# Hybrid encoder step on one core: the gate chain in five pieces, the memory values later, and the last sums of squares by accumulating transfers

## Chip, cores and metric

One core of a Trainium2 chip. The metric is the time of one execution in microseconds of the device. Six engines matter: PE (TensorE: matmuls, with PEld its weight loads), DVE (VectorE), ACT (ScalarE), POOL (GpSimd) and SP (SyncE), which issues most transfers.

## What is computed

One inference step of a one-layer encoder for 512 prompt frames and 32 sample frames, T = 544 columns, D = 2048, all in float32. Cut to what matters here:

```python
z = rmsnorm(x) @ w_in                        # gb, gc, hin, q, k, v and 8 forget gates
logf = log_sigmoid(z[..., o6:] + b_f)        # cumulated over time, enters the scores
x += concat(rmsnorm(gb * conv(gc * hin)), rmsnorm(attention(q, k, v, logf))) @ w_out
mk, mv = split(rmsnorm(mem) @ w_xkv)         # 256 memory tokens
x += softmax(rmsnorm(x) @ w_xq @ mk.T * scale) @ mv @ w_xo
x += square(relu(rmsnorm(x) @ w_up)) @ w_down
y = rmsnorm(x)
```

Prompt and sample frames have their own caches; new keys, values, gates, convolution rows and memory keys and values are outputs too.

## The kernel before

Activations stand with features on the partitions and the 544 columns along the free axis, in two halves of 272. Every float32 matmul is made of three: a tile is rounded by ScalarE to `hi` (float32r), VectorE subtracts to get `lo` (`split`, L82), and hi·hi, hi·lo and lo·hi are added in PSUM. Weights come raw from HBM by SyncE (`raw`), in blocks of 128 x 1024, and are split on the way (`whi`, `wlo`, tags `hi` and `lo`, four buffers each).

The input projection (22 pairs of output blocks) and the first MLP matrix (32 pairs) use `seven` (L240): seven products of 24 matmuls, on sums of weight blocks (`combine`, VectorE, names `sum`) and on sums of column halves made beforehand by `operands` (L199: `b11`, `b21`, `b22`, `t1` to `t4`), in the order b11, t1, t2, b22, t3, b21, t4. Product b11 goes to the PSUM tile X (`mmx`), which ScalarE copies out (`p15`, L259) before t2 may accumulate further in it; t1 goes to Y (`mmy`, copied at L263).

The order of each engine's queue is the order of the program, but for two helpers: `combine` and `operand` (the split of weights) are placed 40 instructions earlier, and `rstd` at the place that a scheduler finds for it. `rstd` (L168) makes the reciprocal root of a mean square: a matmul with a constant matrix sums the tile `acc` over the partitions (`ssq`), ScalarE takes a logarithm and an exponential, and four VectorE steps refine it (`nt`, `rstd`). `square` (L185) has ScalarE square a tile, and VectorE add it to `acc` (`accumulate`, L159).

Stages, in order: head; 22 pairs of the input projection, the first ten of them convolution blocks (`hr`, `gc`, `gb`), the others keys, queries and values; attention beside half 0 of `w_out`; half 1; memory keys (L777 to 789) and values (L790 to 804); the four heads' queries and scores (L902 to 913), values (`x_transpose`, `x_values`); `w_xo` in 16 units of 128 outputs (`xo_done`, L936: add to the residual `x2r`, store, square into `acc_3`, scale by the gain, and at every second unit `operands` for the MLP); `rb_3` of `acc_3` (L1010); 32 `seven`s up; down; final norm.

Places that the change touches:

- The gates: `chain_logf` (L357) after pair 0, with the transposes `turn_logf` after pair 1. ScalarE's part of it is `e` (L365), `lf` (L367), `neg` (L380) and `ncs` (L386); VectorE's has a reciprocal (L369) and two scans (L378, L383). It uses eight rotating tiles of `tmp`.
- `rb_c`, the norm of the convolution group, made right after the last `gb` (L487).
- The memory values, made right after the keys, and each head's transposes and values (`sb`, `sc`) between the queries of the next.
- The weights of `w_xo`, split as each block is needed (L979).
- The last residual's sum of squares:

```python
        dve.tensor_tensor(two(x), two(x), ps[:, :, :TH], ALU.add)
        sp.dma_start(x3d[m], x)
        square(x, acc_3, m == order[0])
```

Of the kernel before, what the change touches and what calls it, by code (L numbers as in the profile page):

```python
# [15 lines left out]
D = 2048  # L16
# [25 lines left out]
def hybrid_step(  # L42
# [125 lines left out]
    def rstd(acc, dim, width=T, early=0):  # L168
        with tc.high_priority(offset=early):
# [29 lines left out]
    def operands(x, b11, ts, tags):  # L199
        hi, lo = two(b11)[:, 0], two(b11)[:, 1]  # L200
        split(hi, lo, x[:, 0])
        t = ts.rearrange("p (a b c) -> p a b c", a=2, b=2)
        x4 = x.rearrange("p (a b) c -> p a b c", a=2)
        dve.tensor_tensor(t[:, :, 0], x4[:, :, 1], x4[:, 0], ALU.subtract)
        for a in range(2):
            dve.tensor_tensor(t[:, a, 1], x[:, 3 - a], t[:, 0, a], ALU.subtract)
        o = {"b11": (hi, lo)}
        o["b21"], o["b22"] = both(x[:, 2:], tags[1])
        o["t1"], o["t2"] = both(t[:, 0], tags[0])
        o["t3"], o["t4"] = both(t[:, 1], tags[2])  # L210
        return o
# [28 lines left out]
    def seven(pl, ops, ws, out, scale, mid, prefetch):  # L240
# [25 lines left out]
        product(X, w, "t2", False)  # L266
        act.activation(u23[:, 0], X, AF.Copy)
# [89 lines left out]
    def chain_logf(z16):  # L357
        z, lf, e, w = tmp("z"), tmp("lf"), tmp("e"), tmp("w")
        z, lf, e, w = z[:8, :T], lf[:8, :T], e[:8, :T], w[:8, :T]
        for a in range(2):  # L360
# [13 lines left out]
        cum, lfs = tmp("cum"), tmp("lfs")  # L374
        act.dma_start(lfs[:8, :PAST], clogf)
# [98 lines left out]
    for i, pair in enumerate(pairs):  # L474
# [315 lines left out]
    ps = mm_tile()  # L790
    for p in range(8):
        hi, lo = weights(w_xv[p])
        for kk in range(2):
            k = 2 * p + kk
            c = slice(512 * kk, 512 * kk + 512)
            for t in range(2):
                d = slice(128 * t, 128 * t + 128)
                for n, (x, w) in enumerate(((mem[k][0], hi), (mem[k][0], lo), (mem[k][1], hi))):
                    pe.matmul(ps[:, t], x[:, d], w[:, c], start=k == 0 and n == 0, stop=k == KD - 1 and n == 2)  # L799
    for t in range(2):  # L800
        mf = tmp("mv")[:, :512]
        dve.tensor_scalar(mf, ps[:, t], rcol[:, t:t + 1], None, ALU.mult)
        pool.dma_start(o_mv[128 * t:128 * t + 128], mf)
        split(mvs[t][0], mvs[t][1], mf)
# [28 lines left out]
    def x_scores(h, q):  # L833
        P = xp.tile([128, 4, NMEM], F32, tag="P", name="xP")
# [19 lines left out]
    def x_transpose(h, P):  # L854
        PT = []
        for kt in range(2):
# [3 lines left out]
            hi = xp.tile([128, SEQ], F32R, tag=f"pth{kt}", name="xpth")  # L860
            lo = xp.tile([128, SEQ], F32R, tag=f"ptl{kt}", name="xptl")
# [4 lines left out]
    def x_values(h, PT):  # L866
# [51 lines left out]
    acc_3 = new_acc()  # L918
# [17 lines left out]
    def xo_done(m, ps):  # L936
# [337 lines left out]
```

## Time and profile before

| | us |
|---|---|
| three runs | 2391.26, 2392.85, 2392.91 (median 2392.85) |
| the profiled execution | 2392.07 |
| its span | 2390.3 |
| PE busy | 2325.7 (97%) |
| DVE busy | 2017.8 (84%) |
| ACT busy | 1303.1 (55%) |
| POOL busy | 197.0 (8%) |

The mean granted clock of TensorE is 0.988 of full speed. TensorE's busy time counts overlapped matmuls once; a matmul of 128 x 272 takes a new place every 0.125 us at the full clock. The gap between TensorE's busy time and the span is 64.6 us.

### The profile page before, as it was taken

Reading aid. Unit: us, or ns where it says so; the run is one execution under the profiler, and the core shown is the slowest. Engines: PE = TensorE matmul, PEld = TensorE weight load, DVE = VectorE, ACT = ScalarE, POOL = GpSimd, SP = SyncE. Lnnn points to the kernel's source line nnn. Section 1 sums busy time; section 2 is a strip of 40 time slices with the busy share of each in tenths; the row PEclk is TensorE's granted clock in tenths of the full one; section 3 lists DMA queues with packets and bytes.
Section 4 is the critical chain, followed back from the end, with each engine's and each line's share of the span. In section 5 each row is a group of like instructions: output and inputs, shape, how many; then the busy total and the mean of one; then the engine's idle time right before and its main releaser. Section 6 shows DMA issues by size and latency. Waiting matters only on the chain.

```text
span 2390.3 us, 47513 instructions
## 1 busy us (share of the span) xinstructions
PE 2325.7 (97%) x18147; PEld 2295.4 (96%) x18147; DVE 2017.8 (84%) x3561; ACT 1303.1 (55%) x2524; POOL 197.0 (8%) x382
## 2 busy tenths in 40 slices
PE   8799999999999999899999999999999999999997
PEld 8699989999999998799999999999999999999997
DVE  9888988886767665989999999998598898888887
ACT  8345445554555444756666665666255555555555
POOL 0000011112300000001111111111000000000000
PEclk9899999999999999899999999999999999999999
DMA  5323345548715453446565556565956546646524
GB/s 176 106 99 125 110 133 157 162 153 317 235 62 166 139 168 127 158 142 203 190 203 186 184 194 204 191 201 172 351 191 237 174 152 237 214 131 219 177 84 137
DMA packets 160484, 416.34 MB, mean 174 GB/s; under 512 B 19384, under 2 KB 24368, under 8 KB 160256
## 3 DMA queue, kind: packets, MB, share of 16 engines
q1 hardware_dynamic: 110752, 313.87, 39.2%
q0 software_dynamic: 44000, 90.52, 12.0%
q10 hardware_dynamic: 5504, 8.93, 1.0%
q8 instruction: 142, 2.33, 0.4%
q14 instruction: 86, 0.70, 0.1%
HBM read 319.91 MB, written 93.33 MB: 173 GB/s over the span
## 4 chain that ended last, share of the span: by engine, by line
PE 91%; DVE 5%; DMA 1%; ACT 1%; issue 1%; DVEq 0%; SPq 0%; ACTq 0%
PE mmx L247 26%; PE dx L1083 14%; PE mmy L247 13%; PE mm L120 13%; PE mm L1083 11%; PE mmz L247 7%; PE mm L1177 2%; PE mm L785 1%; PE mm L799 1%; DVE wlo L85 1%; DVE opl L85 1%; PE s L532 1%; PE mm L311 1%; PE h L311 1%; PE o L588 1%
## 5 line engine op out<-in xcount | busy, mean ns | idle before, releaser
L84 ACT ACTIVATE whi<-raw 128x512 fp32r<-128x512 f32 x668 | 420.6, 632 | 498.8 <-PE mmx L247 97.1
L84 ACT ACTIVATE whi<-sum 128x512 fp32r<-128x512 f32 x656 | 409.9, 630 | 432.4 <-PE mmx L247 205.3
L85 DVE TENSOR_TENSOR wlo<-raw,whi 128x512 fp32r<-128x512 f32 x668 | 457.0, 688 | 137.6 <-ACT whi L84 125.6
L85 DVE TENSOR_TENSOR wlo<-sum,whi 128x512 fp32r<-128x512 f32 x656 | 439.6, 685 | 77.8 <-ACT whi L84 74.9
L247 PE MATMUL mmx<-oph,whi 128*128 128x272 f32 x1296 | 375.3, 290 | 20.1 <-ACT p L259 20.1
L247 PE MATMUL mmx<-oph,wlo 128*128 128x272 f32 x1296 | 375.9, 290 | 2.3 <-DVE wlo L85 2.3
L247 PE MATMUL mmx<-opl,whi 128*128 128x272 f32 x1296 | 373.8, 288 | 0.0
L1083 PE MATMUL dx<-f,whi 128*128 128x272 f32 x1792 | 344.4, 288 | 0.0
L1083 PEld LDWEIGHTS dx<-f,whi 128*128 128x128 f32 x1792 | 281.6, 188 | 0.0
L247 PEld LDWEIGHTS mmx<-oph,whi 128*128 128x128 f32 x1296 | 246.1, 190 | 21.2 <-ACT p L259 21.2
L1083 PE MATMUL mm<-f,whi 128*128 128x272 f32 x1344 | 259.6, 288 | 0.0
L1083 PE MATMUL dx<-f,wlo 128*128 128x272 f32 x896 | 258.5, 289 | 0.0
L247 PE MATMUL mmy<-oph,whi 128*128 128x272 f32 x864 | 250.9, 290 | 1.4 <-ACT whi L84 1.4
L247 PE MATMUL mmy<-oph,wlo 128*128 128x272 f32 x864 | 250.0, 289 | 0.7 <-DVE wlo L85 0.7
L247 PE MATMUL mmy<-opl,whi 128*128 128x272 f32 x864 | 249.4, 289 | 0.0
L247 PEld LDWEIGHTS mmx<-oph,wlo 128*128 128x128 f32 x1296 | 245.4, 189 | 2.7 <-DVE wlo L85 2.7
L247 PEld LDWEIGHTS mmx<-opl,whi 128*128 128x128 f32 x1296 | 245.5, 189 | 0.0
L1083 PEld LDWEIGHTS mm<-f,whi 128*128 128x128 f32 x1344 | 210.8, 188 | 0.0
L1083 PE MATMUL mm<-f,wlo 128*128 128x272 f32 x672 | 193.4, 288 | 0.0
L1083 PEld LDWEIGHTS dx<-f,wlo 128*128 128x128 f32 x896 | 168.9, 189 | 0.0
L247 PEld LDWEIGHTS mmy<-oph,whi 128*128 128x128 f32 x864 | 164.0, 190 | 2.0 <-ACT whi L84 1.8
L247 PE MATMUL mmx<-b,whi 128*128 128x272 f32 x864 | 165.0, 288 | 0.0
(381 smaller groups left out, 5175.2 us busy)
## 6 DMA issues: line engine op xcount, KB each, us to landing
raw<-in_w_up SPq DMA_DIRECT2D x128, 512.0 KB, 3.9
raw<-in_w_dn SPq DMA_DIRECT2D x112, 512.0 KB, 4.3
f<-fd SPq DMA_DIRECT2D x196, 272.0 KB, 5.7
fd<-form POOLq DMA_DIRECT2D x168, 272.0 KB, 4.0
raw<-in_w_in SPq DMA_DIRECT2D x88, 512.0 KB, 3.8
raw<-in_w_out SPq DMA_DIRECT2D x32, 512.0 KB, 4.3
raw<-in_w_ends SPq DMA_DIRECT2D x20, 512.0 KB, 4.1
kq<-hl POOLq DMA_DIRECT2D x32, 256.0 KB, 3.0
```

The source lines that it names most:

```text
L84: act.activation(hi, src, AF.Copy)
L85: dve.tensor_tensor(lo, src, hi.bitcast(F32), ALU.subtract)
L120: pe.matmul(ps[a], w, two(x)[:, a], start=first and n == 0, stop=last and n == 2)
L247: pe.matmul(ps, a[:, c], x, start=first and j == 0 and n == 0, stop=j == 7 and n == 2, skip_group_check=not first)
L311: pe.matmul(ps[a], w[:, c], xs[a][q], start=j + i == 0 and n == 0, stop=j + i == 8 and n == 2)
L532: pe.matmul(s[:, :N], q[a][:, c], k[b][:, :N], start=n == 0, stop=n == 2)
L588: pe.matmul(o[:, 128 * kt:], a[:, c], b, start=kt == 0 and n == 0, stop=False)
L785: pe.matmul(ps[:, 0, :NMEM], w[:, c], x, start=k == 0 and n == 0, stop=k == KD - 1 and n == 2)
L799: pe.matmul(ps[:, t], x[:, d], w[:, c], start=k == 0 and n == 0, stop=k == KD - 1 and n == 2)
L1083: pe.matmul(ps, a[:, c], f[:, x], start=first and j == 0 and n == 0, stop=j == 3 and n == 2, skip_group_check=not first)
L1177: pe.matmul(ps, w[:, c], two(x)[:, a], start=k == 0 and j == 0, stop=k == 3 and j == 2)
```

## The change

1. `operands` issues the same instructions in another order.
2. The gates' chain is cut into `gate_open`, `gate_exp`, `gate_log` and `gate_close`, called after pairs 0, 1, 2 and 4. `neg` is made by VectorE instead of ScalarE, the load of the cached gates (`lfs`) is issued one piece earlier, and the tiles come from other pools (one for `z`, one of tag `acc` for `e`, one of tag `hl` for `w`).
3. `rb_c` is made after pair 13 instead of pair 9.
4. The memory values (`mem_values`) are made after all four heads' queries and scores; all transposes and values of the heads follow them, in an order in which the transposes run a head ahead.
5. Four of the eight `w_xo` blocks are loaded and split inside `mem_values` (`presplit`).
6. `acc_3` becomes two tiles. The first unit of each is squared straight into it by ScalarE; the other 14 squares go to a tile `sq`, and GpSimd issues a transfer that adds `sq` to `acc_3[i]` in SBUF (`accum_op=ALU.add`). `rstd` sums a list of tiles in PSUM (one more `ssq` matmul for each half).
7. `rb_3` is asked for inside the first hidden `seven`, through the new argument `between`, after product t2.
8. The tiles of `plain`, `forms` and the heads' outputs come from a pool `ring` of three, which lives from the cross attention to the end of the first MLP matrix.

```diff
--- before.py
+++ after.py
     def rstd(acc, dim, width=T, early=0):
+        accs = acc if isinstance(acc, list) else [acc]
         with tc.high_priority(offset=early):
             rt = npool.tile([128, T], F32, tag="rstd", name="rstd", bufs=3)
             nt = tmp("nt")
@@ -173,7 +174,8 @@
             for c in range(0, width, half):
                 d = slice(c, c + half)
                 ps = aux("ssq")
-                pe.matmul(ps[:, :half], inv[dim], acc[:, d], start=True, stop=True)
+                for n, t in enumerate(accs):
+                    pe.matmul(ps[:, :half], inv[dim], t[:, d], start=n == 0, stop=n == len(accs) - 1)
...
+    gate = {}
+
+    def gate_open(z16):
+        z = gate["z"] = npool.tile([128, T], F32, tag="rstd", name="z", bufs=3)[:8]
+        e = gate["e"] = new_acc()[:8]
         for a in range(2):
             pz = aux("pz")
             pe.matmul(pz[:8, :TH], sel16, two(z16)[:, a], start=True, stop=True)
             dve.tensor_scalar(two(z)[:, a], pz[:8, :TH], vec[:8, BF:BF + 1], None, ALU.add)
         dve.scalar_tensor_tensor(e, z, -1.0, z, ALU.mult, ALU.min)
+
+    def gate_exp():
+        e = gate["e"]
+        w = gate["w"] = pj.tile([128, T], F32, tag="hl", name="w", bufs=4)[:8]
         act.activation(e, e, AF.Exp)
         dve.tensor_scalar(w, e, 1.0, None, ALU.add)
+        gate["lfs"] = tmp("lfs")
+        act.dma_start(gate["lfs"][:8, :PAST], clogf)
...
+    def gate_log():
+        z, e, w = gate["z"], gate["e"], gate["w"]
+        lf = tmp("lf")[:8, :T]
         act.activation(lf, w, AF.Ln)
         dve.scalar_tensor_tensor(e, w, -1.0, e, ALU.add, ALU.subtract)
         dve.reciprocal(w, w)
...
-        dve.tensor_tensor_scan(cum[:8, :SEQ], one, lf[:, :SEQ], 0.0, ALU.mult, ALU.add)
-        neg = tmp("neg")[:8, :SEQ]
-        act.activation(neg, cum[:8, :SEQ], AF.Copy, scale=-1.0)
-        pool.dma_start(ncd, neg)
-        cs = tmp("cs")
-        dve.tensor_tensor_scan(cs[:8, :LS], ones.to_broadcast([8, LS]), lfs[:8, :LS], 0.0, ALU.mult,
+        cum = gate["cum"] = gate["z"]
+        neg = gate["e"]
+        dve.tensor_tensor_scan(cum[:, :SEQ], one, lf[:, :SEQ], 0.0, ALU.mult, ALU.add)
+        dve.tensor_scalar(neg[:, :SEQ], cum[:, :SEQ], -1.0, None, ALU.mult)
+        pool.dma_start(ncd, neg[:, :SEQ])
...
+    def gate_close():
+        cs = gate["w"]
...
+        turn_logf(gate["cum"])
...
-        if i == 0:
-            cum = chain_logf(z16)
-        if i == 1:
-            turn_logf(cum)
+        if i < 5:
+            (lambda: gate_open(z16), gate_exp, gate_log, lambda: None, gate_close)[i]()
         if n2 == "gb" and j2 == 7:
             pool.dma_start(o_conv, newc)
+        if i == len(pairs) - 9:
             rb_c = rstd(acc_c, DC)
...
         product(X, w, "t2", False)
+        if between:
+            between()
...
+    def mem_values():
...
+            if 2 <= p < 6:
+                wos.append(presplit(w_xo[p - 2]))
...
+    def presplit(src):
+        raw = raw_block(src, None, "raw")
+        his, los = [], []
+        for c in range(0, 1024, 512):
+            hi, lo = slot("B", F32R, "woh")[:, :512], slot("C", F32R, "wol")[:, :512]
+            split(hi, lo, raw[:, c:c + 512])
+            his.append(hi)
+            los.append(lo)
+        return Parts(his), Parts(los)
...
     for h in range(HX):
         qs[h] = evac_xq(h, xq(h))
-        if h == HX - 1:
-            Pss = xs_scores()
-            sa(h)
-            sb(h - 1)
-            sc(h - 1)
+        sa(h)
+    Pss = xs_scores()
+    mem_values()
+    for h in range(HX):
+        if h < 3:
+            o = ring("o")
+            ox.append((flat(o[:, 0]), flat(o[:, 1])))
         else:
-            sa(h)
-            if h < HX - 2:
-                sb(h)
-                sc(h)
+            ox.append([npool.tile([128, T], F32R, tag="rstd", name="o", bufs=3) for n in range(2)])
...
-    acc_3 = new_acc()
+    acc_3 = [new_acc(), new_acc()]
...
-        square(x, acc_3, m == order[0])
         j, i = m % 8, m // 8
+        if j == 0:
+            act.activation(acc_3[i], x, AF.Square)
+        else:
+            sq = tmp("sq")[:, :T]
+            act.activation(sq, x, AF.Square)
+            pool.dma_start(acc_3[i], sq, accum_op=ALU.add)
...
+    sb(0)
     PTs = samp_transpose(xp, Pss, NMEM)
+    sb(1)
+    sc(0)
     osx = samp_values(xp, PTs, cmvt, None)
+    sb(2)
+    sc(1)
     ot = samp_out(osx)
     for i in range(HX):
         split(ox[i][0][:, SEQ:], ox[i][1][:, SEQ:], ot[:, 32 * i:32 * i + 32])
-    order = [m for j in range(8) for m in (j, j + 8)]
-    wo = None
+    sb(3)
+    sc(2)
...
-            wo = weights(w_xo[i // 2])
+            wo = wos[i // 2] if i < 8 else weights(w_xo[i // 2])
...
-    rb_3 = rstd(acc_3, D)
+    rb_3 = []
...
-                    lambda: fetch_up(i + 1))
+                    lambda: fetch_up(i + 1), (lambda: rb_3.append(rstd(acc_3, D))) if i == 0 else None)
```

In ScalarE's queue, the place is the pair after `chain_logf` was called (pair 1 of the input projection). Before:

```order
L187 ACTIVATE sq<-h_1117 128x544
L84 ACTIVATE whi<-sum 128x512 x2
L365 ACTIVATE e<-e 8x544
L367 ACTIVATE lf<-w 8x544
L375 DMA lfs<-in_clogf 8x256
L380 ACTIVATE neg<-cum 8x512
L386 ACTIVATE ncs<-cs 8x288
L259 ACTIVATE p_1436<-mmx 128x272
L263 ACTIVATE p_1436<-mmy 128x272
L84 ACTIVATE whi<-sum 128x512 x2
```

Now:

```order
L261 ACTIVATE p_1409<-mmx 128x272
L84 ACTIVATE whi<-sum 128x512 x2
L265 ACTIVATE p_1409<-mmy 128x272
L375 ACTIVATE acc<-acc 8x544
L84 ACTIVATE whi<-sum 128x512 x2
L271 ACTIVATE u_1410<-mmx 128x272
L84 ACTIVATE whi<-raw 128x512 x2
L84 ACTIVATE whi<-raw_1353 128x512 x2
L275 ACTIVATE u_1410<-mmx 128x272
L84 ACTIVATE whi<-raw 128x512 x2
L84 ACTIVATE whi<-sum 128x512 x2
L378 DMA lfs<-in_clogf 8x256
```

`p` and its twin, which empty the banks X and Y, stood behind five steps of the gates, `neg` and `ncs` with them; now one exponential (`acc<-acc`, which is `e`) stands between two copies, behind X's own, and the load of the cached gates comes half a pair later.

In VectorE's queue, the place is the `w_xo` stretch, some two units of it. Before:

```order
L938 TENSOR_TENSOR x2r<-x2r,mm 128x544
L163 TENSOR_TENSOR acc<-acc,sq 128x544
L85 TENSOR_TENSOR b_12421<-x,b_12421 128x272
L85 TENSOR_TENSOR wlo<-raw,whi 128x512
L163 TENSOR_TENSOR acc<-acc,sq 128x544
L204 TENSOR_TENSOR ts<-x 128x2x272
L85 TENSOR_TENSOR opl<-x,oph 128x544
L206 TENSOR_TENSOR ts<-x,ts 128x272
L938 TENSOR_TENSOR x2r<-x2r,mm 128x544
L206 TENSOR_TENSOR ts<-x,ts 128x272
L85 TENSOR_TENSOR opl<-ts,oph 128x544
```

Now:

```order
L85 TENSOR_TENSOR b_12425<-x,b_12425 128x272
L207 TENSOR_TENSOR ts<-x 128x2x272
L85 TENSOR_TENSOR opl<-x,oph 128x544
L208 TENSOR_TENSOR ts<-x,ts 128x272
L975 TENSOR_TENSOR x2r<-x2r,mm 128x544
L211 TENSOR_TENSOR ts<-x,ts 128x272
L85 TENSOR_TENSOR opl<-ts,oph 128x544 x2
L975 TENSOR_TENSOR x2r<-x2r,mm 128x544
L85 TENSOR_TENSOR b_12511<-x,b_12511 128x272
```

The rows of L163, one for each unit, and the split of this block's weights (`wlo<-raw`) are gone; the residual's add (`x2r`) and the splits for the MLP are left.

In the same stretch ScalarE's queue, with numbers and waits, reads now:

```order
L982 ACTIVATE sq_12387<-x2r_12273 128x544 [waits DMAHW6_49,DMASW3_49,DVE_49]
L84 ACTIVATE oph_12345<-ts_12340 128x544 [waits DVE_49]
L986 ACTIVATE x_12390<-x2r_12273,vec_78 128x544
L84 ACTIVATE oph_12354<-ts_12340 128x544 [waits DVE_49]
L84 ACTIVATE b11_12425<-x_12390 128x272 [waits Activation_49]
L982 ACTIVATE sq_12421<-x2r_12307 128x544 [waits DMAHW7_49,DMASW4_49,DVE_49]
L986 ACTIVATE x_12390<-x2r_12307,vec_78 128x544
L84 ACTIVATE oph_12435<-x_12390 128x544 [waits Activation_49]
L84 ACTIVATE oph_12431<-ts_12426 128x544 [waits DVE_49]
L982 ACTIVATE sq_12473<-x2r_12359 128x544 [waits DMAHW1_49,DMASW5_49,DVE_49]
```

The semaphores named DMASW count GpSimd's transfers. Each square `sq` waits for one of them, that of the square two units back (the same one of the two buffers).

In TensorE's queue, the place is the end of the first hidden block's first product (`mmx`) and the start of its second (`mmy`). Before:

```order
L247 MATMUL mmx<-b_12805,whi 128x272 x2
L247 MATMUL mmx<-b_12805,wlo 128x272
L247 MATMUL mmx<-b_12897,whi 128x272 x2
L247 MATMUL mmx<-b_12897,wlo 128x272
L176 MATMUL ssq<-acc,inv_88 128x272 x2
L247 MATMUL mmy<-oph,whi 128x272
L247 MATMUL mmy<-opl,whi 128x272
L247 MATMUL mmy<-oph,wlo 128x272
```

Now:

```order
L249 MATMUL mmx<-b_12799,whi 128x272 x2
L249 MATMUL mmx<-b_12799,wlo 128x272
L249 MATMUL mmx<-b_12891,whi 128x272 x2
L249 MATMUL mmx<-b_12891,wlo 128x272
L249 MATMUL mmy<-oph,whi 128x272
L249 MATMUL mmy<-opl,whi 128x272
L178 MATMUL ssq<-acc,inv_88 128x272 x3
L249 MATMUL mmy<-oph,wlo 128x272
L249 MATMUL mmy<-oph,whi 128x272
```

`ssq` stood directly behind the first product; now two matmuls of the second precede it, and the fourth `ssq` stands at the end of that product. Its waits are for the last two accumulating transfers, one for each buffer.

## Rows read from the trace of the kernel before

**Rows 1.** The page's list of engines: busy us, share of the span, instructions.
```profile
PE 2325.7 (97%) x18147; PEld 2295.4 (96%) x18147; DVE 2017.8 (84%) x3561; ACT 1303.1 (55%) x2524; POOL 197.0 (8%) x382
```

**Rows 2.** Waits of PE: whom it waited for, us in total, times, longest us.
```profile
PE mmx L247 <- ACT p L259: 20.1, 5, 15.3
...
PE ssq L176 <- DVE acc L163: 6.9, 2, 5.3
...
PE xo L872 <- ACT xP L847: 1.2, 1, 1.2
```

**Rows 3.** Stretches: us; busy us (instructions) PE, PEld, DVE, ACT, POOL; PE clock; DMA; GB/s.
```profile
99.80:120.40 20.60, 5.31 (x27) 5.30 (x27) 15.53 (x19) 4.21 (x9) 2.01 (x4) 0.59 0.23 74
307.80:319.43 11.63, 6.28 (x31) 5.80 (x31) 9.92 (x19) 4.59 (x10) 1.06 (x2) 0.71 0.42 138
120.40:141.50 21.10, 21.10 (x170) 20.93 (x170) 17.98 (x36) 9.91 (x18) 0.00 (x0) 1.00 0.29 98
141.50:162.60 21.10, 21.10 (x170) 21.10 (x170) 19.27 (x29) 11.08 (x20) 1.09 (x2) 1.00 0.39 130
...
847.28:869.47 22.19, 22.19 (x98) 18.15 (x98) 14.07 (x23) 10.92 (x19) 0.54 (x1) 1.00 0.63 200
...
928.40:943.47 15.07, 12.54 (x88) 9.33 (x88) 9.64 (x25) 6.91 (x21) 0.00 (x0) 1.00 0.13 45
943.47:998.42 54.95, 50.25 (x365) 49.01 (x364) 51.51 (x91) 42.19 (x73) 0.00 (x0) 0.94 0.70 236
998.42:1023.19 24.77, 18.45 (x103) 17.05 (x102) 22.10 (x36) 11.88 (x24) 0.00 (x0) 0.79 0.17 61
1254.97:1276.03 21.06, 21.06 (x170) 21.06 (x169) 19.70 (x33) 12.88 (x25) 3.69 (x7) 1.00 0.60 193
```

**Rows 4.** Timeline of ACT, 96 to 122 us: start, us, instruction, [idle before, releaser].
```profile
113.68 0.63 ACT L380 ACTIVATE neg<-cum 8x512 f32<-8x512 f32 x1 [9.71 <-DVE cum L378]
...
114.68 0.37 ACT L259 ACTIVATE p<-mmx 128x272 f32<-128x272 f32 x1
```

**Rows 5.** Timeline of DVE, the same stretch.
```profile
97.74 0.48 DVE L363 TENSOR_SCALAR z<-pz,vec 8x272 f32<-8x272 f32 x1
...
102.86 0.42 DVE L366 TENSOR_SCALAR w<-e 8x544 f32<-8x544 f32 x1
...
105.59 3.53 DVE L369 RECIPROCAL w<-w 8x544 f32<-8x544 f32 x1
...
114.80 0.45 DVE L387 SCALAR_TENSOR_TENSOR ncs<-cs,ncs 8x288 fp32r<-8x288 f32 x1 [0.51 <-ACT ncs L386]
```

**Rows 6.** Groups of DVE, 943.47 to 998.42: count, busy us, mean ns, idle before.
```profile
L938 DVE TENSOR_TENSOR x2r<-x2r,mm 128x544 f32<-128x544 f32 x15 | 10.7, 713 | 2.0 <-PE mm L120 1.9
L163 DVE TENSOR_TENSOR acc<-acc,sq 128x544 f32<-128x544 f32 x14 | 10.0, 716 | 0.0
...
L85 DVE TENSOR_TENSOR wlo<-raw,whi 128x512 fp32r<-128x512 f32 x12 | 8.2, 683 | 0.0
```

**Rows 7.** Groups of ACT, the same stretch.
```profile
L187 ACT ACTIVATE sq<-x2r 128x544 f32<-128x544 f32 x15 | 9.8, 654 | 1.3 <-DVE x2r L938 1.2
```

**Rows 8.** Timeline of PE, 996 to 1026 us.
```profile
1003.05 1.08 PE L176 MATMUL ssq<-acc,inv 128*128 128x272 f32 x4
...
1014.98 0.59 PE L247 MATMUL mmx<-oph,wlo 128*128 128x272 f32 x1 [1.97 <-DVE wlo L85]
```

**Rows 9.** Timeline of DVE, the same stretch.
```profile
1010.59 0.78 DVE L179 TENSOR_TENSOR nt<-rstd 128x272 f32<-128x272 f32 x2
```

**Rows 10.** Transfers by kind: queue, count, KB each, median us to landing.
```profile
x2r<-x2d SPq DMA_DIRECT2D x16, 272.0 KB, 3.9
x3d<-x2r SPq DMA_DIRECT2D x16, 272.0 KB, 2.8
```

**Rows 11.** Issues of the tile fd, min/median/max ns, and its transfers' landing.
```profile
L1008 POOL DMA_DIRECT2D fd<-form x168: 531/531/540, 1079.9 to 1651.1; - x168
...
DMA to landing us min/median/max: 2.3/4.6/10.4
```

More of the change, by code (lines that the diff above doesn't have):

```diff
@@ L203, in operands @@
         x4 = x.rearrange("p (a b) c -> p a b c", a=2)
+        o = {"b11": (hi, lo)}
         dve.tensor_tensor(t[:, :, 0], x4[:, :, 1], x4[:, 0], ALU.subtract)
-        for a in range(2):
-            dve.tensor_tensor(t[:, a, 1], x[:, 3 - a], t[:, 0, a], ALU.subtract)
-        o = {"b11": (hi, lo)}
+        dve.tensor_tensor(t[:, 0, 1], x[:, 3], t[:, 0, 0], ALU.subtract)
+        o["t1"], o["t2"] = both(t[:, 0], tags[0])
         o["b21"], o["b22"] = both(x[:, 2:], tags[1])
-        o["t1"], o["t2"] = both(t[:, 0], tags[0])
+        dve.tensor_tensor(t[:, 1, 1], x[:, 2], t[:, 0, 1], ALU.subtract)
         o["t3"], o["t4"] = both(t[:, 1], tags[2])
@@ L238, in fetch, with seven @@
         return a11, a21, a22, a12, combine(pl, a21, a22, ALU.add)
-    def seven(pl, ops, ws, out, scale, mid, prefetch):
+    def seven(pl, ops, ws, out, scale, mid, prefetch, between=None):
         def product(ps, w, name, first):
@@ L789, in hybrid_step @@
         split(xh_[0][:, h], xh_[1][:, h], mf)
[L790 to L804, printed above, removed]
+    def mem_values():
+        ps = mm_tile()
+        for p in range(8):
+            hi, lo = weights(w_xv[p])
+            for kk in range(2):
+                k = 2 * p + kk
+                c = slice(512 * kk, 512 * kk + 512)
+                for t in range(2):
+                    d = slice(128 * t, 128 * t + 128)
+                    for n, (x, w) in enumerate(((mem[k][0], hi), (mem[k][0], lo), (mem[k][1], hi))):
+                        pe.matmul(ps[:, t], x[:, d], w[:, c], start=k == 0 and n == 0, stop=k == KD - 1 and n == 2)
+            if 2 <= p < 6:
+                wos.append(presplit(w_xo[p - 2]))
+        for t in range(2):
+            mf = tmp("mv")[:, :512]
+            dve.tensor_scalar(mf, ps[:, t], rcol[:, t:t + 1], None, ALU.mult)
+            pool.dma_start(o_mv[128 * t:128 * t + 128], mf)
+            split(mvs[t][0], mvs[t][1], mf)
+    wos = []
+    def presplit(src):
[7 more added lines that the diff above has]
+        return Parts(his), Parts(los)
     x2g = []
@@ L947, in xo_done @@
             ops.append(operands(xgs.pop(j), b11, up.tile([128, 2 * T], F32, tag="sum", name="ts"), "ABC"))
-    ox.append((slot("A", F32R, "oh"), slot("A", F32R, "ol")))
+    order = [m for j in range(8) for m in (j, j + 8)]
+    sb(0)
     PTs = samp_transpose(xp, Pss, NMEM)
+    sb(1)
+    sc(0)
     osx = samp_values(xp, PTs, cmvt, None)
+    sb(2)
+    sc(1)
     ot = samp_out(osx)
@@ L954, in hybrid_step @@
         split(ox[i][0][:, SEQ:], ox[i][1][:, SEQ:], ot[:, 32 * i:32 * i + 32])
-    order = [m for j in range(8) for m in (j, j + 8)]
-    wo = None
+    sb(3)
+    sc(2)
     early = []
     for i in range(2):
-        if i % 2 == 0:
-            wo = weights(w_xo[0])
         ps = mm_tile()
         c = slice(512 * i, 512 * i + 512)
-        early.append((ps, (wo[0][:, c], wo[1][:, c])))
+        early.append((ps, (wos[0][0][:, c], wos[0][1][:, c])))
         xo_part(ps, early[i][1], 0, 3)
         if i == 0:
-            sb(3)
             sc(3)
@@ L1008, in forms @@
                 pool.dma_start(two(fd[i][q]), f[:, n])
-    rb_3 = rstd(acc_3, D)
+    rb_3 = []
     def relu(dst, src, cols):
-        dve.scalar_tensor_tensor(dst, src, 0.0, rb_3[:, cols], ALU.max, ALU.mult)
+        dve.scalar_tensor_tensor(dst, src, 0.0, rb_3[0][:, cols], ALU.max, ALU.mult)
     def fetch_up(i):
@@ L1031, in hybrid_step @@
     up_cm.__exit__(None, None, None)
+    ring_cm.__exit__(None, None, None)
     down_cm = tc.tile_pool(name="down", bufs=1, side="right")
```

37 lines of the change are left out of this document (18 added, 19 removed).

## The prediction

> **What bounds the kernel now.** The first view is the page's list of engines [rows 1]: TensorE is busy for 2325.7 of 2390.3 us, so whatever the change does, its worth is the time in which TensorE stands still or runs slowly; VectorE, at 84%, is the engine that can make it wait. The second view, TensorE's waits by releaser [rows 2], says where: 20.1 us for ScalarE's `p` (15.3 of it in one stall), 6.9 us for VectorE's last sum of squares (5.3 in one stall), and smaller ones such as 1.2 us for `xP`. The third is the table of stretches [rows 3]. Its last row is an undisturbed `seven`: 168 matmuls in 21.06 us at a granted clock of 1.00, so 24 matmuls are worth 3.01 us. Against that pace three places lose time.
>
> - **A, 99.80 to 120.40.** 24 matmuls take 20.60 us; 17.6 us are lost. ScalarE's rows [rows 4] show why: `neg` waits 9.71 us for VectorE's scan `cum`, and `p`, which empties the PSUM bank that TensorE needs, stands behind it in ScalarE's queue. VectorE reaches `cum` late because of the chain ahead of it, a reciprocal of 3.53 us above all [rows 5]. After the stall the granted clock is 0.59 over the stretch, so part of the loss is matmuls at the lower level (1.2 GHz).
> - **B, 307.80 to 319.43.** 24 matmuls and the `ssq` of `rb_c` (4.1 us by pace, with 1.08 for an `ssq` pair as in [rows 8]) take 11.63; 7.5 us are lost while TensorE waits for VectorE's sum of squares.
> - **C, 928.40 to 1023.19.** The attention values lose 2.5 us (TensorE busy 12.54 of 15.07). The `w_xo` stretch has 43.7 us of matmuls (16 units of 24, less the 36 matmuls begun early) in 54.95: 11.3 lost, with VectorE busy for 51.51. The first hidden block up to its fifth product has four products and the `ssq` pair, 13.1 us, in 24.77: 11.7 lost. Together 25.5.
>
> The three hold 50.6 us, which is the ceiling of a gain.
>
> **The change, part by part.**
>
> *Gate chain.* The chain's VectorE work is 13 instructions from 97.74 to 114.80, 11.0 us in sum [rows 5]; `neg` joins them at about 0.42, the duration of `w` in the same group. It is spread over five pairs, and no ScalarE instruction waits for the reciprocal or the scans any more, so the stall behind `neg` goes. What is late next is VectorE itself: in two pairs without gate work it is busy 17.98 and 19.27 of 21.10 us [rows 3], so a pair has 2.5 us to spare on average. The pieces of 1.7, 0.4 and 0.5 us fit; the third piece, from the reciprocal to both scans with `neg`, is 8.9 us and overruns by 6.4. Two products' weights are split ahead (four buffers of halves, 6.0 us), which covers about half of that: I take 3.5 lost there, and 2.3 in the pair where `z` and `e` still stand ahead of a weight sum. Gain 17.6 - 5.8 = **11.8**; bounds 8 (the 6.4 uncovered, and 3.2 beside it) and 17.6 (all covered).
>
> *rb_c four pairs later.* Its sum of squares is long done by then; the two `ssq` cost their 1.08, the four small VectorE steps lie beside matmuls in pairs that have neither convolution nor gate work. Gain **6.8** of 7.5; bounds 5.5 and 7.5.
>
> *Memory values after the scores.* 22.19 us of matmuls now stand between the last scores and the first transposes, and cover the soft-max of the last heads (`xP` in [rows 2]). In exchange the values' own evacuation (`mv`, two times scale, round, subtract) stands directly ahead of the matmuls that read it, with the transposes as cover. I take as much lost there as before: gain **0**, bounds -2 and 2.5.
>
> *w_xo.* Two things leave VectorE: the accumulations (10.0 us for the 14 in the stretch, and a copy of some 0.4) and the `wlo` of blocks 0 to 3, of which 6 of the 12 `wlo` there, 4.1 us, belong to this stretch [rows 6]. Its 51.51 becomes 37.0, below the 43.7 of TensorE; ScalarE's 42.19 [rows 3] loses the matching `whi`, since the squares stay with it [rows 7]. The presplit's eight pairs of `whi` and `wlo` go where VectorE is busy 14.07 of 22.19. In the second half, where weights are still split, VectorE is near parity with TensorE, so a small loss stays: I take 2.8 of 11.3, gain **8.5**, bounds 3 and 10.
>
> This holds only if the accumulating transfers keep pace. Each waits for the one before on its buffer, and ScalarE's square of a unit waits for the transfer two units back; a round is square 0.65 [rows 7], about 0.3 of issue, and the landing time L, and must fit in two units, 6.02 us: free up to L = 5.1. The trace has no accumulating transfer. The nearest rows are plain 272 KB ones [rows 10, 11]: 2.8 and 3.9 us at the median for this stretch's own from SyncE's queue; from GpSimd's, in the MLP, 2.3 at least, 4.6 at the median and 10.4 at worst. An accumulating one has to read two sources, so I take **L = 4.5**, above the loads of the same stretch and about the median of GpSimd's, which its queue is nearest to; both ends, 2.3 and 10.4, stay for the range. The Trainium skill, "DMA: Bandwidth & Descriptors", section "Anatomy of one DMA — SWDGE (gpsimd) path", fits a transfer issued by GpSimd as 2.0 us plus its bytes at 436 GB/s; that is an estimate of 2.6 us for one operand and 3.3 for two, with which the chain would be free with more to spare; the trace's median of 4.6 speaks for more than the fit, and the sum does not use it.
>
> *First hidden block.* The tail is the price: after the last `w_xo` matmul come add (0.71), square (0.65), issue and transfer, about 6.8 us with queueing, before the last accumulation is in. TensorE has b11's 24 and two matmuls of t1 ahead of `ssq`, 3.3 us plus about 0.5 to start: some 3 us of stall. Two more `ssq` cost 1.08 by [rows 8], since the buffers are summed in PSUM. ScalarE's logarithm of it stands ahead of rounding s2, and on VectorE one `nt` step ahead of the sum s2; three more stand behind the sums, where before all of `nt` (from 1010.59, 2.85 us in four double steps like the one shown) came ahead of s3 and of the split that TensorE waited 1.97 us for [rows 8, 9]. By that chain t2 starts about 12 us after the last `w_xo` matmul and the fifth product 18 to 19, against 24.77. Gain **5.5**, bounds -1 and 7.5.
>
> *The rest* (order inside `operands`, pools and tags) moves no work onto the path: the same instructions, with TensorE's first operands ready earlier. Nothing.
>
> Sum: 11.8 + 6.8 + 0 + 8.5 + 5.5 = 32.6. The profiled execution took 2392.07 us, 0.8 below the median of the runs shown, 2392.85. 2392.85 - 32.6 is **2360**.
>
> **Rivals.**
>
> 1. *The accumulating transfers set the pace.* Beyond L = 5.1 each of seven rounds costs L - 5.1, and the tail L - 4.5 more. L = 7 gives 13 + 2.5, so about 2376; no gain is left at L = 9.1, where 8 L - 35.7 - 4.5 reaches 32.6, and the kernel is slower by more than 0.2% from L = 9.7: L = 10.4, the worst landing of `fd`, gives 2403. For it: every landing lies on a serial chain, and landings of 10 us exist. Against: those are transfers queued behind many others, and the stretch's own are at 2.8 and 3.9.
> 2. *Descriptor writing is held up by VectorE.* The same chain, stretched by late issues. GpSimd's issue rows show 531 ns at the median and 540 at most over 168 issues [rows 11] beside a VectorE 94% busy, so it has little for it; 2365 if each issue doubled to 1.06. The Trainium skill, "SBUF — State Buffer", section "Who interferes with whom", says that VectorE instructions in the two-port mode block GpSimd's descriptor writing; by that rule the issues would stretch, and the rows show none that did.
> 3. *The gate work only moves.* If the convolution pairs have no real slack, the 11 us come back as `wlo` waits in five places: A gains 4 instead of 11.8, 2368.
> 4. *w_xo is bound elsewhere*, by the ping-pong of two PSUM tiles between TensorE and VectorE's add, or by ScalarE: C gains 4 instead of 14, 2370.
> 5. *The change does not do what it says* (the running sum leaves VectorE, but VectorE and ScalarE wait for it as long): that is the end of rival 1, priced there.
>
> **How the numbers follow.** Forecast 0.60; rival 1 with L from 5.1 to 8.5 0.12, from there to 9.7 (within 0.2% of no change) 0.04, beyond 0.06; rival 2 0.03; rival 3 0.08; rival 4 0.07. The range 2348 to 2382 goes from C and A at their good bounds (17.6 + 6.8 + 20 = 44.4) to rival 1 at L = 7.8, with rivals 3 and 4 together, 2378, inside; that leaves out some 0.15. From no change a measurement tells 0.2%, 4.8 us, so faster means under 2388.1. Faster 0.90, same 0.04, slower 0.06.
>
> **What would show it.** Right: TensorE's wait for `p` falls from 20.1 to under 5; the wait for VectorE's `acc` goes; the accumulating transfers land in 4 to 5 us; no square waits for one; VectorE under 40 us in `w_xo`; a wait of some 3 us of `ssq` for a transfer. Wrong: a landing over 5.1 with squares waiting 1 us or more each; `wlo` waits of over 8 us in the third gate pair; `w_xo` above 50 us with VectorE idle.

## The result, and the profile after

The changed kernel takes 2367.45 us (median of four runs, 2366.42 to 2368.22) against 2392.88 before: 25.4 us less, a ratio of 0.9894 with a 95% interval of 0.9877 to 0.9911. The forecast was 2360 in 2348 to 2382: the direction is right and the time lies in the range; the gain is 78% of the 32.6 us that the sum gave.

The page's list of engines after the change answers to [rows 1]:

```profile
PE 2319.0 (98%) x18151; PEld 2288.0 (97%) x18151; DVE 2005.4 (85%) x3546; ACT 1300.3 (55%) x2523; POOL 209.1 (9%) x396
```

TensorE is busy for 6.7 us less although it has more `ssq` matmuls, because fewer of its matmuls run at the lower clock after a stall (the mean granted clock is 0.995 instead of 0.988); the rest of the gain is idle time. Whom TensorE waited for, as in [rows 2]:

```profile
PE mmx L249 <- ACT p L261: 6.0, 4, 2.1
...
PE mm L120 <- DVE x2r L975: 2.5, 2, 2.3
...
PE ssq L178 <- DVE acc L163: 1.5, 1, 1.5
PE xo L913 <- ACT mv L84: 1.2, 1, 1.2
```

The wait of 15.3 us for `p` and that of 5.3 us for the sum of squares are gone. The one of 1.2 us for `mv` is new: the memory values' own evacuation. The stretches after, with the columns of [rows 3] (first those of pairs 1 to 4, then pair 10, the end of memory values and attention values, `w_xo`, and the first hidden block up to its fifth product):

```profile
95.21:118.20 22.99, 21.71 (x169) 21.27 (x169) 22.66 (x41) 10.99 (x20) 1.06 (x2) 1.00 0.36 116
118.20:139.26 21.06, 21.06 (x170) 21.06 (x169) 18.96 (x32) 10.05 (x19) 0.00 (x0) 1.00 0.31 102
139.26:163.28 24.02, 21.89 (x171) 21.24 (x170) 23.99 (x35) 11.57 (x21) 2.09 (x4) 1.00 0.35 113
163.28:187.09 23.81, 21.75 (x174) 21.36 (x172) 22.46 (x44) 11.86 (x22) 2.11 (x4) 1.00 0.35 113
294.16:316.89 22.73, 21.32 (x170) 21.11 (x169) 21.31 (x37) 11.71 (x21) 2.70 (x5) 1.00 0.36 119
907.00:927.20 20.20, 18.95 (x114) 15.42 (x115) 15.57 (x29) 11.56 (x24) 1.08 (x2) 1.00 0.67 228
927.20:977.90 50.70, 47.23 (x365) 45.91 (x363) 38.62 (x69) 35.93 (x63) 10.36 (x12) 1.00 0.93 257
977.90:999.30 21.40, 17.76 (x104) 15.96 (x105) 18.38 (x30) 12.96 (x25) 1.72 (x2) 0.84 0.47 126
```

Four pairs with gate work take 91.88 us where four undisturbed ones take 84.24. `w_xo` takes 50.70 instead of 54.95, with VectorE at 38.62 instead of 51.51, near the 37.0 of the sum; but the share of the DMA engines is 0.93 where it was 0.70, and TensorE, whose 364 matmuls of the stretch are worth 45.7 us at 24 in 3.01 us, is still 5.0 us late. (The prediction's 43.7 is 16 matmuls short: the trace of before has 20 of `w_xo`'s 384 ahead of the stretch and not 36, and the row in [rows 3] says x365, one of them an attention value's.) By the start of each stage in TensorE's timeline the gain of 23.9 us in span comes from pairs 0 to 9 (10.5), pairs 10 to 21 (6.0), `w_xo` (4.5), the first hidden block (3.4) and the attention values (0.4); the loads ahead of the attention took 1 us more. Such stage times have their own scatter, and much of it is the clock: the first hidden block, whose code is the same in the kernel before and in two of the experiments (gate_only and rbc_only), takes 24.8, 22.3 and 22.4 us in the three traces, with nearly the same waits, at a granted clock of 0.79, 0.92 and 0.92. Its row in gate_only:

```profile
989.32:1011.65 22.33, 15.81 (x102) 14.41 (x101) 21.80 (x36) 12.04 (x24) 0.00 (x0) 0.92 0.20 70
```

So the terms are also taken from runs below.

### The profile page after: what moved, and what is told of

Read it like the earlier page. It is cut to its first block, busy times and chain, and to the rows that moved or that the text cites. A ratio compares the mean times of both kernels' runs of the same rounds, so it can differ in the third digit from the quotient of the medians.

```text
span 2366.4 us, 47513 instructions
## 1 busy us (share of the span) xinstructions
PE 2319.0 (98%) x18151; PEld 2288.0 (97%) x18151; DVE 2005.4 (85%) x3546; ACT 1300.3 (55%) x2523; POOL 209.1 (9%) x396
## 4 chain that ended last, share of the span: by engine, by line
PE 76%; issue 15%; DVE 4%; DMA 3%; ACT 1%; POOL 1%; SPq 0%; DVEq 0%; POOLq 0%; ACTq 0%
PE mmx L249 26%; PE dx L1128 14%; PE mmy L249 13%; PE mm L1128 11%; PE mmz L249 7%; PE mm L120 2%; PE mm L1222 2%; DMA kq<-kq 1%; DVE wlo L85 1%; PE mm L315 1%; PE h L315 1%; DMA acc<-sq 1%; DMA kc<-kqs 0%; DVE opl L85 0%; DMA x2r<-x2d 0%
## 5 line engine op out<-in xcount | busy, mean ns | idle before, releaser
L84 ACT ACTIVATE whi<-raw 128x512 fp32r<-128x512 f32 x660 | 415.0, 631 | 490.5 <-PE mmx L249 96.9
L85 DVE TENSOR_TENSOR wlo<-raw,whi 128x512 fp32r<-128x512 f32 x660 | 451.7, 689 | 127.0 <-ACT whi L84 119.0
```

The costliest lines, as they stand in the source:

```text
L84: act.activation(hi, src, AF.Copy)
L85: dve.tensor_tensor(lo, src, hi.bitcast(F32), ALU.subtract)
```

## The experiments

The kernels differ in one or two places from the changed kernel or from the one before. "First block" is the first hidden block up to its fifth product; `w_xo` runs from the last attention value to its end. Both are taken from the start of the stages in TensorE's timeline, of one execution each. The last column is the granted clock of the first block.

| kernel | us, median | w_xo | first block | clock |
|---|---|---|---|---|
| before | 2392.9 | 55.2 | 24.8 | 0.79 |
| changed | 2367.5 | 50.7 | 21.4 | 0.84 |
| dve_add | 2367.1 | 51.3 | 19.4 | 1.00 |
| plain_copy | 2361.9 | 47.6 | 20.0 | 0.91 |
| plain_load | 2368.2 | 52.4 | 20.5 | 0.92 |
| pool_add | 2371.6 | 55.8 | 21.2 | 0.84 |
| half_half | 2364.8 | 47.9 | 21.0 | 0.92 |
| acc_only | 2392.7 | 54.4 | 24.0 | 0.86 |
| no_presplit | 2370.9 | 56.2 | 20.9 | 0.92 |
| mix_late | 2365.6 | 48.7 | 21.2 | 0.92 |
| half_late | 2365.3 | 49.3 | 21.0 | 0.92 |
| half_early | 2363.2 | 48.4 | 18.9 | 1.00 |
| gate_only | 2380.1 | 54.7 | 22.3 | 0.92 |
| rbc_only | 2385.0 | 54.7 | 22.4 | 0.92 |

half_half and half_late have the same code in `w_xo` and differ there by 1.4 us: a smaller difference of `w_xo` between two traces says nothing.

**What the adding transfers are worth.** The theory was the prediction's: VectorE's additions bound `w_xo`, and the transfers took that away. The rival: they give it back elsewhere. First the transfers alone are undone (dve_add):

```diff
-            pool.dma_start(acc_3[i], sq, accum_op=ALU.add)
+            dve.tensor_tensor(acc_3[i], acc_3[i], sq, ALU.add)
```

> The changed kernel, but the 14 squares are added to the two buffers by VectorE instead of by transfers; nothing else differs. My theory (VectorE's adds bound the w_xo stretch; the transfers took that away and gave a part back by late landings): VectorE gets 14 x 0.64 = 9 us back, 1.3 us for each pair of units over TensorE's 6.02 in the second half, so w_xo grows by 3 to 6 us from 50.5, while the last residual load comes on time and the first hidden block loses 2 to 3 us less: 2367 to 2371. Rival 1 (the adds were never the bound, the gain is the presplit and the order): 2363 to 2365, that is faster than the changed kernel, w_xo 48 or less. Rival 2 (the transfers are worth their whole cover): over 2373.

2367.12 us, against 2367.45: no difference. That the time lies at the lower end of the theory's range is chance: `w_xo` is longer by 0.6 us and not by 3 to 6. Then they alone are put into the kernel before, with the two buffers and the two more `ssq` (acc_only):

```diff
-        square(x, acc_3, m == order[0])
+        if j == 0:
+            act.activation(acc_3[i], x, AF.Square)
+        else:
+            sq = tmp("sq")[:, :T]
+            act.activation(sq, x, AF.Square)
+            pool.dma_start(acc_3[i], sq, accum_op=ALU.add)
```

> The kernel before with one part of the change: the last sums of squares go into two buffers by adding transfers (the first unit of each squared straight in, two ssq for each half), all else as before. Theory (VectorE's adds bound w_xo, the adding transfers overfill the DMA engines): VectorE in w_xo falls from 51.5 to about 41, the DMA share there rises from 0.70 to over 0.9 with landings up to 8 us; the gain of the one is mostly eaten by the other and by 1.1 us of ssq and a later last landing: 2388 to 2392. Rival 1 (transfers hide, the adds were the bound): 2384 to 2387. Rival 2 (without the presplit the late landings decide): over 2394.

2392.69 us, ratio 1.0001 (0.9992 to 1.0010), a little above the range of the theory and far from that of rival 1. Both ways round the transfers are worth nothing. VectorE's load did fall, and the stretch did not get shorter; here are its two rows (`w_xo`, first block):

```profile
943.70:998.10 54.40, 47.55 (x367) 46.13 (x365) 42.79 (x76) 40.26 (x71) 10.38 (x12) 1.00 0.98 284
998.10:1022.10 24.00, 17.99 (x104) 16.30 (x105) 21.09 (x35) 12.88 (x25) 1.72 (x2) 0.86 0.36 98
```

VectorE has 42.79 us of 54.40, the DMA engines are full (0.98). One bound was exchanged for another; that the DMA engines are the new one is what the next two runs test.

**Why.** Two runs ask whether it is the adding itself. The same transfers without the addition (plain_copy):

```diff
-            pool.dma_start(acc_3[i], sq, accum_op=ALU.add)
+            pool.dma_start(acc_3[i], sq)
```

> The changed kernel with the same 14 transfers that copy instead of adding, so the sums of squares hold the last unit of each half alone. It shows what the adding itself costs. My theory (an adding transfer holds the DMA engines about twice as long for its bytes, and the DMA engines are full in w_xo, 0.88 and 0.98): landings 3 to 4 us with none over 5.5, no wait of ScalarE's square over 1 us, DMA share 0.8; w_xo 47 to 48.5 instead of 50.5, first hidden block 1 to 3 us shorter: 2361 to 2364. Rival (the stretch's own loads and stores make the landings late, adding costs nothing of its own): landings 3.4 to 8.0 as before and 2366 to 2368.

2361.86 us, 5.6 less, as the theory had it, though landings still reach 6.7 us. And the same plain transfers twice, the second to a place that nobody reads (plain_load):

```diff
-            pool.dma_start(acc_3[i], sq, accum_op=ALU.add)
+            pool.dma_start(acc_3[i], sq)
+            pool.dma_start(spare[m], sq)
```

> The run plain_copy with a second plain transfer of each square, to a spare place in memory: about the DMA work of an adding transfer, without its read and write of one buffer. Only the last units' squares are in the sums. Theory (it is the work on the DMA engines that makes landings late): w_xo back to 50 to 52, DMA share 0.95 or more, 2366 to 2370. Rival (it is the adding transfer's own latency on the chain of one buffer): w_xo 47.5 to 48.5, landings of the first copy as in plain_copy (3.9 median), 2361 to 2363.5.

2368.21 us: the whole of the 5.6 is back, without any addition. The queues in `w_xo` (packets, MB, share of the 16 engines; then the transfers, median us to landing), of the changed kernel:

```profile
q1 hardware_dynamic: 4368, 9.94, 58.7%
q0 software_dynamic: 1548, 3.01, 33.7%
...
x3d<-x2r SPq DMA_DIRECT2D x15, 272.0 KB, 4.6
acc<-sq POOLq DMA_DIRECT2D x12, 272.0 KB, 5.3
```

of plain_copy:

```profile
q1 hardware_dynamic: 4464, 10.11, 66.3%
q0 software_dynamic: 948, 3.33, 17.1%
...
x3d<-x2r SPq DMA_DIRECT2D x15, 272.0 KB, 3.4
acc<-sq POOLq DMA_DIRECT2D x12, 272.0 KB, 3.9
```

Some of these land behind the end of `w_xo`, so what one costs is taken from a stretch that holds all 14. GpSimd's queue from 936 to 990 us in the changed kernel, from 936 to 984 in plain_copy and from 936 to 990 in plain_load:

```profile
q0 software_dynamic: 2016, 3.90, 40.9%
...
q0 software_dynamic: 1120, 3.90, 20.1%
...
q0 software_dynamic: 2240, 7.80, 36.4%
```

40.9% of 54 us for 14 transfers is 1.58 us of all 16 engines each; 20.1% of 48 is 0.69; 36.4% of 54 is 1.40 for a pair, of which the second goes to HBM. An adding transfer of 272 KB holds the engines 2.3 times as long as a plain one, a little longer than two plain ones. With it the other transfers of the stretch are late as well (`x3d` 4.6 against 3.4, and 4.3 in plain_load). So the addition as such is not needed for the loss; plain_load does not separate the load on the engines from the tile that stays occupied until the second transfer has landed, for which ScalarE's squares wait 4.8 us there.

How that reaches TensorE is seen in the changed kernel. GpSimd's issues (ns) and their landing, over all 14, then for the one issued at 960.21 and the one at 962.47:

```profile
L983 POOL DMA_DIRECT2D acc<-sq x14: 850/858/900, 938.3 to 982.2; - x14
...
DMA to landing us min/median/max: 3.4/4.8/8.0
...
DMA to landing us min/median/max: 7.8/7.8/7.8
...
DMA to landing us min/median/max: 7.6/7.6/7.6
```

The first landed at 968.0, the second at 970.1. ScalarE's timeline (squares) and, below, SyncE's:

```profile
943.38 0.66 ACT L982 ACTIVATE sq<-x2r 128x544 f32<-128x544 f32 x1 [2.44 <-DMA acc<-sq]
...
968.03 0.66 ACT L982 ACTIVATE sq<-x2r 128x544 f32<-128x544 f32 x1 [3.14 <-issue]
```

```profile
970.28 0.32 SPq L964 DMA_DIRECT2D x2r<-x2d  x1
...
972.00 0.48 SPq L964 DMA_DIRECT2D x2r<-x2d  x1
```

VectorE's and TensorE's, behind the square of 968.03:

```profile
969.37 0.72 DVE L207 TENSOR_TENSOR ts<-x 128x544 f32<-128x544 f32 x1 [2.56 <-ACT x L986]
...
970.87 0.74 PE L120 MATMUL mm<-o,whi 128*128 128x272 f32 x4 [2.27 <-DVE x2r L975]
```

The square at 968.03 starts just as the transfer of 960.21 lands, which read the tile that it writes; behind it ScalarE is late, then VectorE, then TensorE (its 2.3 us for `x2r` at 970.87). SyncE's load of the 15th unit's residual, at 970.28, stood 4.5 us for the second, because its tile too comes from the pool of six that the squares use; the 16th unit's load, behind it, lands at 979.5, and with it the last operands of the first hidden block. Rival 1's mechanism is there, in six of 14 landings (over 5.1 us) instead of in the median.

**Other ways to add.** GpSimd itself, no transfer (pool_add):

```diff
-            pool.dma_start(acc_3[i], sq, accum_op=ALU.add)
+            pool.tensor_tensor(acc_3[i], acc_3[i], sq, ALU.add)
```

> The changed kernel, but GpSimd itself adds the square to the buffer, no transfer. No row has a GpSimd add; GpSimd is idle there but for its issues. My theory (what is lost in w_xo is lost to late transfers): if one add stays under 3 us, TensorE's pace for a unit, ScalarE and SyncE wait for none of it: w_xo 47 to 48.5, and the last sum is ready sooner: 2360 to 2364. Rival 1 (GpSimd's add is slower than 3 us): the sums lag, each square waits: 2370 or more. Rival 2 (GpSimd and VectorE slow one another): VectorE's x2r and opl rows grow above 0.72 us, w_xo as it is or longer, 2367 to 2375.

2371.63 us, slower than with VectorE, though GpSimd keeps pace at 1.43 us an addition: rival 2, not the theory. The row of `w_xo`, then groups of POOL, and two of DVE, in this run:

```profile
925.30:981.10 55.80, 49.48 (x365) 47.60 (x364) 48.78 (x69) 36.38 (x63) 17.11 (x12) 0.97 0.55 182
...
L983 POOL TENSOR_TENSOR acc<-acc,sq 128x544 f32<-128x544 f32 x12 | 17.1, 1426 | 46.9 <-ACT sq L982 46.9
```

```profile
L207 DVE TENSOR_TENSOR ts<-x 128x544 f32<-128x544 f32 x7 | 7.6, 1088 | 3.8 <-ACT x L986 3.8
...
L85 DVE TENSOR_TENSOR wlo<-raw,whi 128x512 fp32r<-128x512 f32 x6 | 6.3, 1069 | 0.0
```

The same group in dve_add:

```profile
L207 DVE TENSOR_TENSOR ts<-x 128x544 f32<-128x544 f32 x7 | 5.0, 718 | 1.8 <-ACT x L986 1.8
```

VectorE's 69 instructions take 48.78 us, where the changed kernel's 69 take 38.62. The subtractions `ts` take 1088 ns on average instead of 718 where GpSimd adds beside them, and `wlo` 1069 instead of the 683 of [rows 6]; other groups are as fast as before (`opl` from `x` 712 ns, 716 in dve_add). The Trainium skill, "SBUF — State Buffer", section "Who interferes with whom", says that a VectorE instruction with two inputs in SBUF contends with a GpSimd instruction that reads SBUF; the slowed rows agree, and put a number to it.

Half of the additions by each, VectorE those of i = 1 (half_half):

```diff
+            if i:
+                dve.tensor_tensor(acc_3[i], acc_3[i], sq, ALU.add)
+            else:
+                pool.dma_start(acc_3[i], sq, accum_op=ALU.add)
```

> The changed kernel with the squares of the second half of the rows (i = 1) added by VectorE, those of the first half by transfers. My theory: VectorE gets 7 x 0.64 = 4.5 us back and has room for it (38.7 busy of 50.5), the DMA engines lose half of the adding transfers, and the last unit's sum no longer waits for a landing: w_xo 48 to 49.5, first hidden block 1 to 3 us shorter: 2362 to 2365. Rival (w_xo is bound elsewhere): 2366 to 2368. Rival 2 (VectorE is at its limit): 2368 to 2371.

2364.75 us, `w_xo` 47.9: as expected, while the first block is no shorter. Two more runs build `rb_3` only after product b22:

```diff
         product(X, w, "t2", False)
-        if between:
-            between()
         act.activation(u23[:, 0], X, AF.Copy)
         product(Y, operand(s4), "b22", False)
+        if between:
+            between()
```

one of them with VectorE adding for j = 0 to 3 and 7 and transfers for the rest (mix_late),

```diff
-            pool.dma_start(acc_3[i], sq, accum_op=ALU.add)
+            if j < 4 or j == 7:
+                dve.tensor_tensor(acc_3[i], acc_3[i], sq, ALU.add)
+            else:
+                pool.dma_start(acc_3[i], sq, accum_op=ALU.add)
```

> The changed kernel with the squares of rows j = 0 to 3 and 7 added by VectorE (there it has room, or the last landing would be waited for) and only the six of j = 4 to 6 by transfers, and with rb_3 asked for after product b22 instead of t2. Theory: VectorE's adds fit where the weights are presplit (4.85 + 1.28 against 6.02 for a pair of units), the transfers are few enough to land in time, the last sum is on time, and the nt step no longer stands ahead of the sum s2: w_xo 47 to 48, first block to its fifth product 18 to 19.5 instead of 21.4: 2359 to 2363. Rival (VectorE is late in the first half): w_xo 50, 2363 to 2366.

the other with the additions of half_half (half_late):

> The run half_half with rb_3 asked for after product b22 instead of t2, so that VectorE's first nt step and ScalarE's logarithm no longer stand ahead of the sum s2 and its rounding. Theory: w_xo 47.9 as in half_half, first block to its fifth product 19.5 to 20.5 instead of 21.1: 2362 to 2364.5. Rival (that block is bound by VectorE's backlog before the sum s1, which does not move): 2364 to 2366.

2365.60 and 2365.29: both theories miss. The rival of half_late holds; mix_late's time lies in its rival's range, but its `w_xo` is not at 50. `rb_3`'s place is not what bounds the first block. In half_half (first fence) TensorE waits 2.7 us for the rounding of s1, the block's first sum of weights, which VectorE makes only behind the last unit's operands. Asking for the block's weights one unit earlier (half_early, second fence)

```diff
+        if i == KD - 1:
+            nxt = fetch_up(0)
...
-    nxt = fetch_up(0)
```

> The run half_half with the first hidden block's weights taken up before the last unit of w_xo instead of after it, so that VectorE makes the sum s1 and its split ahead of the last unit's operands. Theory (the first block is bound by what stands ahead of s1 on VectorE: TensorE waited 2.7 us for the rounding of s1): that wait falls under 1 us, first block to its fifth product 18 to 19.5 instead of 21.1, w_xo within 0.7 of 47.9: 2361 to 2363.5. Rival (the last unit's operands are then late instead, for the products t1 and t2): 2364 to 2366.

```profile
PE mmy L249 <- ACT whi L84: 3.6, 2, 2.7
```

```profile
PE mmy L249 <- ACT whi L84: 1.1, 1, 1.1
```

gives 2363.24 us, a ratio of 0.9878 (0.9862 to 0.9894), the first block 18.9: the wait for s1 is gone, and the clock stays at 1.00. By medians it is 4.2 us below the changed kernel; the two intervals overlap, so that it is faster is likely and not settled.

**The other parts.** The gates' pieces alone (part 2 of the change) and `rb_c` alone (part 3), each in the kernel before; then the changed kernel without the presplit:

```diff
-        if i == 0:
-            cum = chain_logf(z16)
-        if i == 1:
-            turn_logf(cum)
+        if i < 5:
+            (lambda: gate_open(z16), gate_exp, gate_log, lambda: None, gate_close)[i]()
```

> The kernel before with the gates' chain cut into five pieces alone. Theory (nothing of the chain stands ahead of ScalarE's copy any more, VectorE takes its work in the slack of five pairs): 10.5 to 12 us faster, 2380.5 to 2382; first ten pairs of the projection 10.5 to 12 shorter, nothing else changed. Rival (the later place of rb_c was needed for part of it): 8 or less.

```diff
+        if i == len(pairs) - 9:
             rb_c = rstd(acc_c, DC)
```

> The kernel before with rb_c four pairs later alone. Theory: the eleventh pair falls from 29.7 to 22.7 us and the fifteenth grows by about 0.9 for the ssq: 6.0 faster, 2386 to 2387. Rival (the wait moves with it): 2390 or more.

```diff
-            if 2 <= p < 6:
-                wos.append(presplit(w_xo[p - 2]))
...
-            wo = wos[i // 2] if i < 8 else weights(w_xo[i // 2])
+            wo = weights(w_xo[i // 2])
```

> The changed kernel without the presplit: the weights of w_xo are loaded and split as each block is needed, as before; memory values, transfers and all else as changed. Theory (the presplit is what gives VectorE, ScalarE and the DMA engines room in the first half of w_xo; the transfers alone are worth nothing): w_xo back to 54 to 55, memory values about 1 shorter: 2370 to 2373. Rival (the order of transposes and values, or the transfers, made the gain in w_xo): 2367 to 2369.

gate_only takes 2380.06 us, 12.6 less than before (ratio 0.9942, 0.9929 to 0.9956); rbc_only 2384.99, 7.7 less (0.9969, 0.9956 to 0.9982); together 20.3, and 5.1 of the change's 25.4 are left for all else. Without the presplit the changed kernel takes 2370.93, 3.5 more, with `w_xo` at 56.2 (the slowest run of the changed kernel is 1 us below the fastest of this one): the presplit is what is left of the gain in that stretch. no_presplit lies in its expected range; gate_only and rbc_only lie 0.4 and 1.0 us below theirs.

## Why the prediction was right, point by point

- **The gate chain**, 11.8 predicted: 12.6 by the run of that part alone, 10.5 by the stages of the changed kernel's trace (pairs 1 to 4 alone give 12.3; pair 0 takes 1.7 more than before, though its code is the same in dve_add and takes 24.2 us there instead of 25.8: its granted clock is 0.93, and 1.00 in dve_add). What was to stay, 5.8 us: pairs 1 to 4 take 7.6 us over four undisturbed ones, 1.7 of it a loss in pair 4 that the kernel before has too. Right, in size and in place: 1.9 stayed in the pair where `z` and `e` stand (2.3 taken) and 3.0 in that of the third piece (3.5 taken).
- **rb_c**, 6.8 predicted: 7.7 by its run, 6.0 by the trace. Right.
- **Memory values**, 0 predicted: 0.4 by the trace, with the new 1.2 us for `mv` as named.
- **w_xo**, 8.5 predicted: 4.5. This step failed, at two places. About half of what is missing is a miscount, 43.7 us of matmuls for 45.7: 9.3 us were lost there and not 11.3, all three places together held 48.6 and not 50.6, and with the 2.8 left that the step takes, the gain would have been 6.5. The other half is the transfers. VectorE fell to 38.6, near the 37.0 worked out. The step "free up to L = 5.1", with "I take L = 4.5", is what did not hold: it gave the transfers a landing time of their own, taken from plain transfers, and asked only whether one fits in a round. The median, 4.8, would have fitted. What the runs showed instead is a load: each adds 1.6 us of all 16 DMA engines to a stretch that already held them at 0.70, so that landings spread from 3.4 to 8.0 and the residual's loads and stores became late with them. The row for it was there, the DMA column of the `w_xo` stretch in [rows 3], and was not used. That SyncE's load would wait for a transfer, through the shared pool of tiles, was not named either.
- **First hidden block**, 5.5 predicted: 3.4 by the trace of before, 1.0 against the two other traces with the same code; the 2.4 between them is the clock. The stall of some 3 us before `ssq` did not come. In its place TensorE waits inside the first product for the operands of the last unit, whose residual came late:

```profile
982.03 0.39 PE L249 MATMUL mmx<-b,whi 128*128 128x272 f32 x1 [1.21 <-ACT b L84]
983.96 0.60 PE L249 MATMUL mmx<-b,whi 128*128 128x272 f32 x1 [1.54 <-DVE b L85]
```

  The granted clock of the block is 0.84. In the kernels in which VectorE adds a part, s1 behind the last unit's operands is the wait; the chain through `rb_3` that the step followed is not the one that binds there, as mix_late and half_late show.
- **Rivals.** Rival 2 did not come about: GpSimd's issues take 858 ns when they add and 546 when they copy, beside the same VectorE. Rival 3 did not. Rivals 1 and 4 are each true in part: `w_xo` is bound elsewhere, by the DMA engines, which rival 4 did not name. By the number alone the forecast is not told from rivals: 2367.45 is nearer to the 2368 of rival 3 and the 2370 of rival 4 than to 2360. The price of rival 2, 2365, does not follow from the prediction's own rule: a round with 0.53 more still fits in 6.02.

- **The signs.** Of those for right, VectorE under 40 us came; the wait for `p` fell to 6.0, not under 5 (4.8 of its 20.1 lay outside the one stall); 1.5 us of the wait for `acc` are left; landings are at 4.8 in the median, but spread; squares did wait; no `ssq` matmul stood 3 us for a transfer. Of the three for wrong, one came, `w_xo` at 50.7 us with VectorE idle for 12 of them, and one came once, a landing of 7.8 us with a square waiting 3.1 for it. `wlo` waits in the third gate pair did not.

A and B were thus what was sure, 18.6 predicted and 20.3 measured; C was to give 14, and 5.1 were left for it and all else. That the time lies in the range owes as much to the range's width, which held rivals 3 and 4, as to the sum: its part C was wrong in mechanism and in size.

## What to carry to other kernels

Work that is moved from an engine to transfers is paid for in DMA engine time: look up the DMA share of the stretch that it goes into, and count an adding transfer as two plain ones or a little more. Before a wait in the middle of an engine's queue is shortened, see what else is queued behind it; cutting a serial chain into pieces, spread over stages with slack, gave half of this change's gain with no work removed. A tile pool that is shared by transfers and loads ties them together: one late landing held up a load that had nothing to do with it.

## What the runs showed of the hardware

An adding transfer of 272 KB within SBUF takes GpSimd 858 ns to issue where a plain one takes 546, and all 16 DMA engines 1.58 us where a plain one takes 0.69. The Trainium skill, "DMA: Bandwidth & Descriptors", section "Anatomy of one DMA — SWDGE (gpsimd) path", gives 2.6 us for a plain one of this size as an estimate from its fit; the fastest plain copy here landed in 2.4 us and agrees, the median of 3.9 beside the stretch's other transfers does not, and for adding ones the measured 4.8 decides. GpSimd adds two tiles of 128 x 544 in 1.43 us; 12 such additions lengthen the work of VectorE's 69 instructions beside them from 38.6 to 48.8 us.
